# A transformer stack of two blocks on one core: small gate rows made later, context loaded later, queries and keys of the second block prepared apart, one gMLP input projected late

## The chip, the cores and the metric

The kernel runs on one core of a Trainium2 chip. TensorE multiplies, VectorE, ScalarE and GpSimd do the rest, SyncE issues the DMAs; the engines run side by side, each its own instructions in order, and wait for one another by semaphores. The metric is the device time in microseconds (us) from a launch to its end. GpSimd has next to no work in this kernel.

## The reference

All values are float32; `x` has 256 tokens of width 1024. `first_block` is one layer:

```python
h = rmsnorm(x, norm1_g)
(hg_q, hg_f, hg_i, hg_g, ml_qk, ml_v, ml_if, ml_o, mb_z, mb_xbc, mb_dt, gate_pre) = split(h @ w_in)
y_hg = rmsnorm(hgrn2_scan(silu(hg_q), log_f, hg_i)) * silu(hg_g)
qk   = silu(causal_dwconv(ml_qk, ml_conv_w, ml_conv_b))
y_ml = rmsnorm(mlstm_scan(q_m, k_m, ml_v, i_pre, log_sigmoid(ml_f))) * sigmoid(ml_o)
dt   = softplus(mb_dt + mb_dt_bias)
y_mb = rmsnorm((ssd_scan(xs, dt, A, Bm, Cm) + D * xs) * silu(mb_z))
x = x + (gates[0] * (y_hg @ w_hg) + gates[1] * (y_ml @ w_ml) + gates[2] * (y_mb @ w_mb)) @ w_out
u_g, u_v = split(causal_dwconv(rmsnorm(x) @ w_up, ffn_conv_w, ffn_conv_b))
x = rmsnorm(x + (silu(u_g) * u_v) @ w_down)
```

`second_block` has two layers, with a context `ctx` of 256 more tokens that the last layer only reads:

```python
sh1, sc1, g1, sh2, sc2, g2 = modulation(c, w_ada[i], b_ada[i])        # and the same for ctx
h  = rms_norm(x) * (1 + sc1) + sh1;   hc = the same of ctx
a_z, bq, bk, bv, cq, ck, cv = split_proj(h @ w_in[i])
u, v  = split(gelu(a_z));  out_a = u * (w_s @ rms_norm(v) + b_s)      # gated MLP over chunks of 128
out_b = window_attn(rope(rms_norm(bq)), rope(rms_norm(bk)), bv, keys and values of ctx, sink)
out_c = rms_norm(diff_attn(rope(rms_norm(cq)), rope(rms_norm(ck)), cv, keys and values of ctx))
x = x + g1 * (concat(out_a, out_b, out_c) @ w_out[i])
x = x + g2 * conv_ffn(rms_norm(x) * (1 + sc2) + sh2)
```

In layer 0 the context goes through the same steps (attention only to itself).

## The kernel before

**Weights.** Every float32 operand is split in two parts of the multiplier's format, high and low, and a product is three matmuls (high by high, high by low, low by high; `mm3`, L409). `weight` (L388) brings a weight tile of 128 x 1024 by DMA (`raw`, four buffers), ScalarE casts its high part (`wh`, L393) and VectorE subtracts the low part (`wl`, L395), three buffers each. `gemm_ws` (L422, tile `psg`) is then 24 matmuls of 128 x 256; `gemm_xs` (tile `psx`, L439 to 441) has the tokens as the stationary side, takes two weight tiles and does 24 matmuls for each block of 128 tokens.

**What sets the order.** The Python code only emits instructions. A scheduler with pools of buffers puts each engine's instructions in a row: in the order of the code where data and buffers allow it by its own estimate of times, else what is ready. Two streams of work are merged by generators: `run_ratio(a, b, n)` takes `n` steps of `b` for each step of `a`.

**First block.** After norm and split of `x`, `proj_a` projects the HGRN2 inputs; beside it `hgrn_core` works by chunks (tiles `hb`, `lnk`, `E`, `AT`, `psl`). `small_rows` (L782) makes softplus and its running sum for the SSD branch: an absolute value and an exponential on ScalarE, and 17 VectorE steps on 128 x 256 (a reciprocal, seven steps of a series at L796, a scan). It is called before `run_ratio(seq(pa, proj_b(), proj_c()), ...)`, with the load of `win` (the window mask, 256 KB) and its cast `winb` behind it. `proj_b` (L931) then runs eight `mqk` gemms, each with a convolution (ScalarE one tap, VectorE three, `cv`, L923) and a silu (`mq`), four pairs of `mv` weights, and more. The MLP `ffn` calls `hook1(j)` once per item `j`; from item 9 on it takes steps of `context_norm`: `prepare(0)` (load of layer 0's parameters `plt`, tables `ct...`, `st...` for the rotation) and the context's first norm. The modulation of layer 0 (`ada`, tiles `psada`, `arow`, `psat`) comes in quarters in between; `context_norm` first runs what is left of it.

**Second block.** `unit` (L1416) projects one input by name: `kv`, `ck` (keys, values), `cq`, `bq0`, `bq1` (queries), `cv` (values of the differential attention), `av` and `au` (the two inputs of the gated MLP; gelu on ScalarE at the evacuation). `qk_part(c)` (L1452) takes the two token blocks of `c` (0 is x, 1 the context): squares on ScalarE, sums on VectorE, Newton steps for the inverse root (`qny`, `qnt`), rotation (`rot`), scaling, then transposes on TensorE (`pst`) and the split into `qkh` and `qkl`. `attention(tiles, age)` (L1662) has eight items for each block of 128 tokens: four pairs of heads of the window kind, four of the differential kind. An item is scores (`psc`, three matmuls per head, 512 keys), maximum on VectorE, exponential on ScalarE (`Pp`), `age` items later the transposes (`psc<-ct,Pp`) and their copy (`PT`), one item after that the values (`pso`). Layer 1 does all projections first, then `gmlp(0)`, attention over blocks 1 and 0 with `age` 3, then `out_proj` (eight gemms over the eight k-tiles: 0, 1 from the gated MLP, 2 to 5 from the window heads, 6, 7 from the differential heads).

## Time and profile before

| | |
|---|---|
| runs before | 1729.18 us (median of 3: 1727.62 to 1729.49) |
| profiled run | 1728.11 us |
| its span, first to last instruction | 1726.3 us |
| mean granted clock of TensorE | 0.991 |
| TensorE busy | 1680.2 us (97%) |
| VectorE busy | 1422.8 us (82%) |
| ScalarE busy | 943.0 us (55%) |

The shares of busy time are means over stages with different limits, so stretches of 6 to 30 us are read one by one below. PE is TensorE's matmuls, PEld its weight loads (beside the matmuls), DVE VectorE, ACT ScalarE, SP SyncE. A row "PEld a <- DVE b" means that the weight load for `a` waited for `b`; the matmul behind it waits about as long. The overlap of neighbouring VectorE instructions (the next starts some 0.08 us before the last one's end) makes a row of them shorter than the sum of their durations.

### The profile page before, as it was taken

What the parts mean: (1) busy time and instruction counts of PE and PEld (TensorE: products, weight loads), DVE (VectorE), ACT (ScalarE), POOL (GpSimd) and SP (SyncE); (2) the same over time, 40 slices, a digit from 0 to 9 for tenths busy, and PEclk for the clock granted to TensorE, in tenths of its full rate; (3) what the DMA queues carried; (4) which work ended last, traced back from release to release, by engine and by line L of the source; (5) the groups of instructions that cost most, each with busy time, mean ns of one, the idle gap of its engine ahead of it and who ended that gap; (6) DMA issues with size and microseconds to landing.
All of it is one profiled execution on the core that took longest, in us unless ns stands there. A gap on an engine that the chain in (4) does not pass through costs nothing.

```text
span 1726.3 us, 31575 instructions
## 1 busy us (share of the span) xinstructions
PE 1680.2 (97%) x12334; PEld 1529.8 (89%) x12334; DVE 1422.8 (82%) x2788; ACT 943.0 (55%) x1661; POOL 0.2 (0%) x4
## 2 busy tenths in 40 slices
PE   7999999999999999999999999999999998899999
PEld 7999998889898999989877988888888996799999
DVE  8987977668789987876788899999997868688776
ACT  7655644444456665666777553431244555576454
POOL 0000000000000000000000000000000000000000
PEclk9999999999999999999999999999999999999999
DMA  8545454536665677764311546657753542046564
GB/s 264 162 151 156 137 159 121 150 111 213 206 212 165 194 234 224 218 203 147 99 50 52 169 138 184 186 170 237 242 165 110 170 134 63 1 144 196 177 193 135
DMA packets 80645, 278.01 MB, mean 161 GB/s; under 512 B 9072, under 2 KB 13808, under 8 KB 80240
## 3 DMA queue, kind: packets, MB, share of 16 engines
q1 hardware_dynamic: 80496, 275.99, 52.1%
q8 instruction: 97, 1.59, 0.4%
q14 instruction: 52, 0.43, 0.1%
HBM read 274.91 MB, written 1.05 MB: 160 GB/s over the span
## 4 chain that ended last, share of the span: by engine, by line
PE 84%; DVE 10%; ACT 3%; DMA 2%; issue 1%; SPq 0%; ACTq 0%; DVEq 0%
PE psg L414 20%; PE psg L417 20%; PE psg L416 20%; PE psx L439 3%; PE psx L441 3%; PE psx L440 3%; DVE wl L395 3%; PE psc L1568 2%; PE psl L894 1%; PE psc L1607 1%; ACT wh L393 1%; PE pso L1629 1%; PE pso L1626 1%; DMA raw<-w 1%; ACT Pp L1587 1%
## 5 line engine op out<-in xcount | busy, mean ns | idle before, releaser
L393 ACT CAST wh<-raw 128x1024 fp32r<-128x1024 f32 (+1 forms) x439 | 453.3, 1037 | 514.3 <-PE psg L416 419.0
L395 DVE TENSOR_TENSOR wl<-raw,wh 128x1024 fp32r<-128x1024 f32 (+1 forms) x439 | 528.2, 1206 | 136.6 <-ACT wh L393 133.6
L414 PE MATMUL psg<-XH,wh 128*128 128x256 f32 (+1 forms) x1272 | 396.3, 314 | 4.7 <-ACT wh L393 3.8
L417 PE MATMUL psg<-XH,wl 128*128 128x256 f32 (+1 forms) x1272 | 395.0, 313 | 4.7 <-DVE wl L395 4.7
L416 PE MATMUL psg<-XL,wh 128*128 128x256 f32 (+1 forms) x1224 | 384.6, 315 | 0.9 <-DVE XL L1331 0.5
L414 PEld LDWEIGHTS psg<-XH,wh 128*128 128x128 f32 x1272 | 240.3, 190 | 23.3 <-ACT wh L393 5.9
L417 PEld LDWEIGHTS psg<-XH,wl 128*128 128x128 f32 x1272 | 240.6, 190 | 21.3 <-DVE wl L395 5.7
L416 PEld LDWEIGHTS psg<-XL,wh 128*128 128x128 f32 x1224 | 231.9, 190 | 17.6 <-issue 1.1
L414 PE MATMUL psg<-xh,wh 128*128 128x256 f32 x720 | 208.2, 289 | 1.3 <-ACT xh L400 1.3
L417 PE MATMUL psg<-xh,wl 128*128 128x256 f32 x720 | 205.3, 285 | 2.6 <-DVE wl L395 2.6
L416 PE MATMUL psg<-xl,wh 128*128 128x256 f32 x720 | 205.7, 286 | 0.6 <-DVE xl L401 0.6
L414 PE MATMUL psg<-hh,wh 128*128 128x256 f32 (+1 forms) x592 | 178.6, 303 | 0.2
L416 PE MATMUL psg<-hl,wh 128*128 128x256 f32 (+1 forms) x592 | 178.3, 302 | 0.0
L417 PE MATMUL psg<-hh,wl 128*128 128x256 f32 (+1 forms) x592 | 178.2, 302 | 0.0
L414 PEld LDWEIGHTS psg<-xh,wh 128*128 128x128 f32 x720 | 137.8, 191 | 4.9 <-issue 2.9
L417 PEld LDWEIGHTS psg<-xh,wl 128*128 128x128 f32 x720 | 137.7, 191 | 4.9 <-DVE wl L395 3.2
L416 PEld LDWEIGHTS psg<-xl,wh 128*128 128x128 f32 x720 | 138.1, 192 | 1.8 <-issue 1.0
L414 PEld LDWEIGHTS psg<-hh,wh 128*128 128x128 f32 x592 | 111.0, 188 | 7.3 <-ACT hh L400 1.1
L416 PEld LDWEIGHTS psg<-hl,wh 128*128 128x128 f32 x592 | 111.2, 188 | 5.7 <-DVE hl L401 0.2
L417 PEld LDWEIGHTS psg<-hh,wl 128*128 128x128 f32 x592 | 111.1, 188 | 5.1
L439 PE MATMUL psx<-wh,XH 128*128 128x256 f32 x384 | 110.2, 287 | 1.3 <-ACT wh L393 0.8
L441 PE MATMUL psx<-wl,XH 128*128 128x256 f32 x384 | 109.3, 286 | 0.6 <-DVE wl L395 0.4
(445 smaller groups left out, 3181.7 us busy)
## 6 DMA issues: line engine op xcount, KB each, us to landing
raw<-w SPq DMA_DIRECT2D x238, 512.0 KB, 4.1
raw<-wb SPq DMA_DIRECT2D x197, 512.0 KB, 4.3
araw<-w SPq DMA_DIRECT2D x56, 512.0 KB, 4.3
raw<-w SPq DMA_DIRECT2D x16, 384.0 KB, 3.3
raw<-wb SPq DMA_DIRECT2D x8, 384.0 KB, 4.0
xres<-xT SPq DMA_DIRECT2D x16, 128.0 KB, 4.3
ccb<-pcb SPq DMA_DIRECT2D x2, 1024.0 KB, 5.4
plt<-pl SPq DMA_DIRECT2D x2, 588.0 KB, 4.2
```

Of the source, the lines that this page charges most:

```text
L393: S.copy(wh[:, 0:sz], raw[:, 0:sz])
L395: V.tensor_tensor(wl[:, 0:sz], raw[:, 0:sz], wh[:, 0:sz], ALU.subtract)
L414: T.matmul(o, wh[:, k], xh, start=(first and k == 0), stop=False)
L416: T.matmul(o, wh[:, k], xl, start=False, stop=False)
L417: T.matmul(o, wl[:, k], xh, start=False, stop=(last and not late and k == nk - 1))
L439: T.matmul(o, xh, wh[:, k % 4], start=(k == 0), stop=False)
L440: T.matmul(o, xl, wh[:, k % 4], start=False, stop=False)
L441: T.matmul(o, xh, wl[:, k % 4], start=False, stop=(k == 7))
L894: T.matmul(ps[:, a, t], E[:, o:o + 128], E[:, o:o + 128], start=True, stop=True)
L1568: T.matmul(ps[e][:, 0:A.nk], q_[d, jq, A.tq], k_[d, jk, kk], start=(n == 0), stop=(n == 2 and not mask))
L1587: S.activation(out=p[:, 0:A.nk], in_=o, func=AF.Exp, scale=ss[:, A.t, h:h + 1], bias=nm, accum_out=sums[:, c:c + 1])
L1607: T.transpose(ps[:, n], p[:, b * 128:(b + 1) * 128], ident)
```

## The change

- **Start.** `small_rows` is called in `proj_b` ahead of the fifth `mqk` gemm, with its rows in another pool. `win` is loaded and cast in two halves at items 6 and 7 of the first MLP. The second gate gemm's result is scaled after the norm's split.
- **Context.** `cx` is loaded at item 4 of the first MLP and the parameters of layer 0 at item 9, each held back by a small ScalarE copy from that item's `av`; a quarter of the modulation is taken at items 12, 15 and 18. In the first MLP's opening the weight of the next item is requested one step earlier.
- **Queries and keys.** `qk_part(c, which)` does the queries or the keys of `c`; sums, Newton steps and transposes are separate (the rows of `qkh` are in another order, so that the transposes of a part are together). Layer 0 takes keys first. Layer 1 takes x's queries, then the context's keys, then x's keys; its first four steps run during `kv` and `ck`.
- **gMLP of layer 1.** `av` is copied out and gets its gelu in one instruction afterwards. The `au` gemms, their gelu and the product come in `gmlp(0, late=True)`, whose steps are taken at items 1, 3, 5, 14, 16 and 17 of attention, which runs with `age` 2. `out_proj` takes its k-tiles in the order 2, 3, 4, 5, 0, 1, 6, 7 in both layers.

```diff
+    fill2 = (1, 3, 5, 14, 16, 17)
...
-    def load_params(pool, spec, src, nm):
+    def load_params(pool, spec, src, nm, gate=None):
...
+        if gate is not None:
+            S.copy(t[:, 0:1], gate[:, 0:1])
         nc.sync.dma_start(out=t, in_=src)
...
-                    hook(j)
+                    hook(j, av)
...
-    uf = [scaled(gemm_ws(0, ("hf", j), graw, 256)) for j in range(2)]
+    uf = [gemm_ws(0, ("hf", j), graw, 256) for j in range(2)]
+    uf[0] = scaled(uf[0])
     normed(xh, xl, x, r, g1[:, 0:8])
+    uf[1] = scaled(uf[1])
...
     def proj_b():
         for j in range(8):
+            if j == 4:
+                small_rows()
...
-    small_rows()
     V.tensor_copy(identb, ident)
     V.tensor_copy(causb, C("causal"))
-    win = mid.tile([128, 512], F32, tag="E", name="win", bufs=4)
-    nc.sync.dma_start(out=win, in_=cstw)
-    V.tensor_copy(winb.rearrange("p a b -> p (a b)"), win)
...
-    cx = load_x(res2, ctxT, tag="cx")
+    cx = res2.tile([128, 8, 256], F32, name="xres", tag="cx")
...
-    def hook1(j):
+    def hook1(j, av):
+
+        gate[0] = av
+        if j in (6, 7):
+            win = tmp.tile([128, 256], F32, tag="t256", name="win", bufs=6)
+            nc.sync.dma_start(out=win, in_=cstw[:, (j - 6) * 256:(j - 5) * 256])
+            V.tensor_copy(winb[:, j - 6], win)
+        if j == 4:
+            S.copy(cx[:, :, 0:1], av[:, 0:8].unsqueeze(2))
+            for k in range(8):
+                nc.sync.dma_start(out=cx[:, k], in_=ctxT[:, k])
         if j >= 9:
             next(cn, None)
+        if j in (12, 15, 18):
+            ada_steps(1)
...
+        QKPART = {"q": (((0, 512, 64), (640, 896, 32)), (((0, 1, 2, 3), 0), ((5, 6), 4))),
+                  "k": (((512, 640, 64), (896, 1152, 32)), (((4, 7, 8), 6),))}
+
+        def qk_part(c, which):
...
+        def gelu(c, which=(0, 1)):
+
+            for a in (A[c][e] for e in which):
+                S.activation(out=a, in_=a, func=AF.Gelu_apprx_tanh)
...
+            if late:
+                for j in range(2):
+                    ps = gemm_ws(ph, ("au", j), lambda k: (XH[:, k, XS], XL[:, k, XS]), 256)
+                    S.copy(AU[:, j], ps[:, 0:256])
+                    yield
+                for _ in gelu(c, (1,)):
+                    pass
+                for b in range(2):
+                    gated(b)
                 yield
...
-                ps = gemm_ws(ph, ("out", m), lambda k: (XH[:, k, o], XL[:, k, o]), 256)
+                ps = gemm_ws(ph, ("out", m), lambda k: (XH[:, k, o], XL[:, k, o]), 256, ks=[2, 3, 4, 5, 0, 1, 6, 7])
...
-            for _ in units(("kv", "ck"), 0, 1):
-                pass
-            run_ratio(seq(units(("av", "au"), 0), units(("cv",), 0, 1)), seq(qk_part(0), qk_part(1)), Knobs.rc)
+
+            qk = seq(qk_part(0, "q"), qk_part(1, "k"), qk_part(0, "k"))
+            run_ratio(units(("kv", "ck"), 0, 1), (next(qk) for _ in range(4)), 2)
+            run_ratio(seq(units(("av",), 0), gelu(0, (0,)), units(("cv",), 0, 1)), qk, Knobs.rc)
             psum(c=6, o=1, s=1)
-            for _ in seq(gmlp(0), attention((1, 0), 3)):
+            gm = gmlp(0, True)
+            for i, _ in enumerate(attention((1, 0), 2)):
+                if i in Knobs.fill2:
+                    next(gm, None)
+            for _ in gm:
                 pass
```

Line numbers move by 4 to 62 (before's L393, L395, L923 are L397, L399, L931 after the change). Three places of the engines' rows:

VectorE in the mLSTM projection, around the `wl` of the first `mv` gemm, before (the first and the last row are the `wl` of the last `mqk` gemm and of the first `mv` gemm):

```order
L395 TENSOR_TENSOR wl<-raw,wh 128x1024
L837 SCALAR_TENSOR_TENSOR mq<-th,cv 128x256
L923 SCALAR_TENSOR_TENSOR cv<-psg,pb1t,cv 128x253
L886 TENSOR_TENSOR E<-E,hq 128x64x4
L923 SCALAR_TENSOR_TENSOR cv<-psg,pb1t,cv 128x254
L884 TENSOR_TENSOR E<-hb 128x128x2
L923 SCALAR_TENSOR_TENSOR cv<-psg,pb1t,cv 128x255
L901 COPY_PREDICATED AT<-ct_125,psl 128x2x256
L923 SCALAR_TENSOR_TENSOR cv<-psg,pb1t,cv 128x253
L837 SCALAR_TENSOR_TENSOR mq<-th,cv 128x256
L923 SCALAR_TENSOR_TENSOR cv<-psg,pb1t,cv 128x254
L395 TENSOR_TENSOR wl<-raw,wh 128x1024
```

After, the last 12 rows ahead of that `wl` (the last row here; the `wl` before it stands 25 rows above the first of these):

```order
L931 SCALAR_TENSOR_TENSOR cv<-psg,pb1t,cv 128x254
L805 SCALAR_TENSOR_TENSOR p<-p,s 128x256
L931 SCALAR_TENSOR_TENSOR cv<-psg,pb1t,cv 128x255
L807 SCALAR_TENSOR_TENSOR SP<-p,z 128x256
L909 COPY_PREDICATED AT<-ct_125,psl 128x2x256
L808 TENSOR_SCALAR z<-SP,acol 128x256
L845 SCALAR_TENSOR_TENSOR mq<-th,cv 128x256
L809 SCALAR_TENSOR_TENSOR CS<-ct_125,z 128x256
L931 SCALAR_TENSOR_TENSOR cv<-psg,pb1t,cv 128x253
L894 TENSOR_TENSOR E<-E,hq 128x64x4
L931 SCALAR_TENSOR_TENSOR cv<-psg,pb1t,cv 128x254
L399 TENSOR_TENSOR wl<-raw,wh 128x1024
```

The small-gate rows (L798 to L809) now stand between the convolution taps, and 35 instructions lie between the two `wl` where there were 10.

TensorE at the end of layer 1's attention, before: scores, transposes and values of the last items, then the output projection (`psg`):

```order
L1568 MATMUL psc<-qkh 128x512 x2
L1568 MATMUL psc<-qkl,qkh 128x512 x2
L1568 MATMUL psc<-qkh,qkl 128x512 x2
L1607 MATMUL psc<-ct,Pp 128x128 x8
L1629 MATMUL pso<-CV,PT 128x128 x12
L1607 MATMUL psc<-ct,Pp 128x128 x4
L1629 MATMUL pso<-CV,PT 128x128 x4
L414 MATMUL psg<-XH,wh 128x256
```

After, at the same place; `psg` is here an `au` gemm:

```order
L421 MATMUL psg<-XL,wh 128x256
L422 MATMUL psg<-XH,wl 128x256
L1664 MATMUL psc<-ct,Pp 128x128 x4
L1686 MATMUL pso<-CV,PT 128x128 x4
L1625 MATMUL psc<-qkl,qkh 128x512 x2
L1625 MATMUL psc<-qkh,qkl 128x512 x2
L419 MATMUL psg<-XH,wh 128x256
L421 MATMUL psg<-XL,wh 128x256
L422 MATMUL psg<-XH,wl 128x256
L1686 MATMUL pso<-CV,PT 128x128 x4
L419 MATMUL psg<-XH,wh 128x256
```

The 48 matmuls of the `au` gemms now stand among the last transposes and values.

ScalarE there, before (up to the squares of the differential heads' output):

```order
L1587 ACTIVATE Pp,dsums<-psc,dnm,ss 128x512 x2
L1643 COPY rsb<-psrs 128x512
L1612 COPY PT<-psc 128x512 x2
L400 CAST XH<-rsb 128x4x128
L1587 ACTIVATE Pp,dsums<-psc,dnm,ss 128x512 x2
L1612 COPY PT<-psc 128x512
L1654 ACTIVATE sqc<-OB 128x256
```

After:

```order
L1669 COPY PT<-psc 128x512
L1644 ACTIVATE Pp,dsums<-psc,dnm,ssq 128x512 x2
L1669 COPY PT<-psc 128x512
L397 CAST wh<-raw 128x1024
L1589 COPY AU<-psg 128x256
L1669 COPY PT<-psc 128x512
L1543 ACT_TABLE_LOAD
L1543 ACTIVATE AU<-AU 128x512
L1711 ACTIVATE sqc<-OB 128x256
L404 CAST XH<-oa 128x256 x2
```

Two weight casts, the copies of the `au` results, a table load and the gelu now stand among the last copies and ahead of the squares.

## Rows read from the trace of the kernel before

**Rows 1.** The page, busy time, the chain that ended last, one costly group

```profile
PE 1680.2 (97%) x12334; PEld 1529.8 (89%) x12334; DVE 1422.8 (82%) x2788; ACT 943.0 (55%) x1661; POOL 0.2 (0%) x4
...
PE 84%; DVE 10%; ACT 3%; DMA 2%; issue 1%; SPq 0%; ACTq 0%; DVEq 0%
...
L395 DVE TENSOR_TENSOR wl<-raw,wh 128x1024 fp32r<-128x1024 f32 (+1 forms) x439 | 528.2, 1206 | 136.6 <-ACT wh L393 133.6
```

**Rows 2.** Stretches: length, busy us (PE, PEld, DVE, ACT, POOL), granted clock, DMA share, GB/s

```profile
100.00:125.00 25.00, 25.00 (x213) 24.90 (x212) 22.52 (x44) 14.73 (x27) 0.00 (x0) 1.00 0.49 148
738.00:752.00 14.00, 11.80 (x64) 7.12 (x64) 9.93 (x19) 11.39 (x20) 0.00 (x0) 0.92 0.75 247
1372.00:1400.00 28.00, 27.77 (x232) 27.60 (x233) 17.08 (x34) 14.55 (x31) 0.00 (x0) 1.00 0.50 151
1430.00:1446.00 16.00, 12.32 (x105) 11.00 (x103) 13.79 (x46) 6.54 (x15) 0.00 (x0) 1.00 0.50 150
1446.00:1475.00 29.00, 26.69 (x208) 18.10 (x210) 20.78 (x58) 18.97 (x43) 0.00 (x0) 0.88 0.01 2
1500.00:1512.00 12.00, 9.11 (x61) 8.51 (x60) 4.95 (x20) 2.90 (x8) 0.00 (x0) 0.86 0.00 0
```

**Rows 3.** Waits, 20 to 30 us: engine, line, releaser, total, times, longest

```profile
PEld psg L417 <- DVE wl L395: 1.6, 1, 1.6
```

**Rows 4.** Waits, 50 to 58 us

```profile
PEld psl L869 <- DVE hq L837: 1.7, 1, 1.7
...
DVE winb L1214 <- DMA win<-cstw: 0.7, 1, 0.7
```

**Rows 5.** Groups of VectorE, 0 to 60 us: count, busy, mean ns, idle before

```profile
L796 DVE SCALAR_TENSOR_TENSOR p<-p,s 128x256 f32<-128x256 f32 x7 | 3.0, 424 | 0.2
...
L791 DVE RECIPROCAL s<-s 128x256 f32<-128x256 f32 x1 | 1.7, 1736 | 0.0
```

**Rows 6.** Timeline of VectorE, mLSTM projection: start, duration, line, tile, shape

```profile
118.57 1.22 DVE L395 TENSOR_TENSOR wl<-raw,wh 128x1024 fp32r<-128x1024 f32 x1
...
123.35 0.48 DVE L923 SCALAR_TENSOR_TENSOR cv<-psg,pb1t,cv 128x254 f32<-128x254 f32 x1
123.75 1.22 DVE L395 TENSOR_TENSOR wl<-raw,wh 128x1024 fp32r<-128x1024 f32 x1
```

**Rows 7.** Timeline of TensorE, first `mv` gemm

```profile
129.44 0.28 PE L441 MATMUL psx<-wl,xh 128*128 128x256 f32 x1
```

**Rows 8.** Waits, 540 to 546 us

```profile
PEld psg L417 <- DVE wl L395: 3.2, 1, 3.2
```

**Rows 9.** Waits, 594 to 605 us

```profile
PEld psg L417 <- DVE wl L395: 1.6, 2, 1.1
```

**Rows 10.** Waits, 738 to 748 us

```profile
PEld psat L538 <- ACT arow L563: 1.9, 1, 1.9
...
PEld psx L439 <- ACT wh L393: 1.4, 1, 1.4
```

**Rows 11.** Waits, 880 to 888 us

```profile
PEld psg L414 <- ACT wh L393: 2.4, 1, 2.4
...
PEld psc L1607 <- DVE Pp L1596: 0.9, 1, 0.9
```

**Rows 12.** Waits, 1436 to 1447 us

```profile
PEld pst L1500 <- DVE qkl L401: 3.1, 3, 1.3
...
PEld psc L1568 <- DVE qkl L401: 1.2, 1, 1.2
```

**Rows 13.** Waits, 1494 to 1506 us

```profile
PE psc L1607 <- DVE Pp L1596: 2.2, 1, 2.2
...
PEld pso L1629 <- ACT PT L1612: 0.9, 1, 0.9
```

**Rows 14.** Timeline of ScalarE, first exponentials of layer 1

```profile
1449.61 1.28 ACT L1587 ACT_TABLE_LOAD   x1 [3.93 <-DVE nm L1585]
1450.90 0.78 ACT L1587 ACTIVATE Pp<-psc,nm,ss 128x512 f32<-128x512 f32 x1
```

More of the change, by code (lines that the diff above doesn't have):

```diff
@@ L407, in gained, with mm3 @@
             V.scalar_tensor_tensor(dst_l[:, k], x[:, k], g[:, k:k + 1], dst_h[:, k], ALU.mult, ALU.subtract)
-    def mm3(o, w, rhs, nk, late=False, first=True, last=True):
+    def mm3(o, w, rhs, nk, late=False, first=True, last=True, ks=None):
         wh, wl = w
-        for k in range(nk):
+        ks = ks or list(range(nk))
+        for k in ks:
             xh, xl = rhs(k)
-            T.matmul(o, wh[:, k], xh, start=(first and k == 0), stop=False)
+            T.matmul(o, wh[:, k], xh, start=(first and k == ks[0]), stop=False)
             if not late:
                 T.matmul(o, wh[:, k], xl, start=False, stop=False)
-            T.matmul(o, wl[:, k], xh, start=False, stop=(last and not late and k == nk - 1))
+            T.matmul(o, wl[:, k], xh, start=False, stop=(last and not late and k == ks[-1]))
         if late:
@@ L662, in ffn @@
                         ps.append(gemm_ws(ph, ("up",) + k, raw[0], raw[3]))
+                    ahead = weight(ph, ("up", raws, 0), 128)
                     us += [raw[1](p) for p in ps[len(us):]]
@@ L678, in ffn @@
                 else:
-                    pg = gemm_ws(ph, ("up", j, 0), part(slice(0, n)), n)
+                    pg = gemm_ws(ph, ("up", j, 0), part(slice(0, n)), n, w=ahead if raw and j == raws else None)
                 ag = conv(pg, j, "ag")
@@ L769, in tile_two_blocks @@
     S.activation(out=lbe, in_=lbe, func=AF.Exp)
+    S.activation(out=sg0, in_=ones, func=AF.Sigmoid)
     lbs = p1.tile([128, 8], F32, name="lbs")
@@ L1346, in context_norm @@
         ada_steps(max(0, 32 - Ada.done))
-        LS[0] = prepare(0)
+        LS[0] = prepare(0, gate[0])
         yield
@@ L1437, in unit @@
                     for i, c in enumerate(cs):
-                        S.activation(out=A[c][1][:, j], in_=ps[:, 256 * i:256 * i + 256], func=AF.Gelu_apprx_tanh)
+                        S.activation(out=A[c][1][:, j], in_=ps[:, 256 * i:256 * i + 256], func=AF.Copy if last else AF.Gelu_apprx_tanh)
                 return
@@ L1441, in unit @@
                     "cv": lambda t, o: S.copy(CV[:, t], o),
-                    "av": lambda t, o: S.activation(out=A[t // 2][0][:, t % 2], in_=o, func=AF.Gelu_apprx_tanh)}[nm]
+                    "av": lambda t, o: S.activation(out=A[t // 2][0][:, t % 2], in_=o, func=AF.Copy if last else AF.Gelu_apprx_tanh)}[nm]
             key = ("bq", int(nm[2])) if nm[:2] == "bq" else (nm,)
@@ L1449, in units @@
                 yield
-        def qk_part(c):
+        QKPART = {"q": (((0, 512, 64), (640, 896, 32)), (((0, 1, 2, 3), 0), ((5, 6), 4))),
+                  "k": (((512, 640, 64), (896, 1152, 32)), (((4, 7, 8), 6),))}
+        def qk_part(c, which):
             toks = (2 * c, 2 * c + 1)
-            full = not (last and c)
+            groups, moves = QKPART[which]
+            ss = S_[which][:, 2 * c:2 * c + 2]
+            n0 = (groups[0][1] - groups[0][0]) // 64
             for t in toks:
-                for c0, c1, d, g0 in (((0, 512, 64, 0), (512, 640, 64, 8), (640, 1152, 32, 10)) if full
-                                      else ((512, 640, 64, 8), (896, 1152, 32, 18))):
+                g0 = 0
+                for c0, c1, d in groups:
                     sq = ap.tile([128, 512], F32, tag="scr", name="sq", bufs=Knobs.scr)
@@ L1496, in qk_part @@
                     g0 += nh
-                for j0, j1 in (((0, 4), (4, 8), (8, 9)) if full else ((4, 5), (7, 9))):
+                if t < 2:
+                    yield
+                for js, to in moves:
+                    n = len(js)
                     ps = PS.s.tile([128, 4, 128], F32, tag="s", name="pst")
-                    for j in range(j0, j1):
-                        T.transpose(ps[:, j - j0], QK[t][:, j * 128:(j + 1) * 128], ident)
-                    split(qkh[:, j0:j1, t * 128:(t + 1) * 128], qkl[:, j0:j1, t * 128:(t + 1) * 128], ps[:, 0:j1 - j0])
+                    for i, j in enumerate(js):
+                        T.transpose(ps[:, i], QK[t][:, j * 128:(j + 1) * 128], ident)
+                    split(qkh[:, to:to + n, t * 128:(t + 1) * 128], qkl[:, to:to + n, t * 128:(t + 1) * 128],
+                          ps[:, 0:n])
@@ L1557, in scores @@
                     d = slice(64 * e, 64 * e + 64)
-                    rows.append((d, i, 4, 2 * i + e, L.nsink[:, 2 * i + e:2 * i + e + 1]))
+                    rows.append((d, i, 6, 2 * i + e, L.nsink[:, 2 * i + e:2 * i + e + 1]))
                 else:
@@ L1577, in scores @@
             for e, (d, jq, jk, h, nsink) in enumerate(rows):
-                c = h if i < 4 else h - 10
+                c = h if i < 4 else h - 8
                 o, nm = ps[e][:, 0:A.nk], nmt[:, c:c + 1]
```

102 lines of the change are left out of this document (56 added, 46 removed).

## The prediction

> **What bounds the kernel now.** I read the page first. TensorE is busy 97% of the span of 1726.3 us and holds 84% of the chain that ended last, VectorE 10% [rows 1]: the time changes only where TensorE stops, or goes on at half clock. Then I listed, for each stretch that the diff touches, which waits TensorE has there and what ended them. Almost all end on VectorE: the low half of a weight, `wl` (439 subtractions, 1.21 us each), or a chain of small vector steps that queued in front of one. A stretch at full speed holds 213 matmuls in 25 us, 0.117 us each, so a gemm of 24 is 2.8 us [rows 1, 2]. A second loss is the clock: where the granted clock of a stretch is below 1, part of it ran at the lower of the two levels (1.2 instead of 2.4 GHz), after TensorE had waited. Its price is the missing share times the length: 0.12 x 29 = 3.5 us in 1446 to 1475, 0.14 x 12 = 1.7 us in 1500 to 1512, 0.08 x 14 = 1.1 us in 738 to 752 [rows 2].
>
> The profiled run took 1728.11 us, 1.07 below the median of 1729.18. The sum is made against the profiled run, and 1.1 us is put back at the end.
>
> **Start (0 to 58 us).** The small-gate rows and the window mask's load and cast leave this place. In front of the third gate gemm TensorE waited 1.6 us for `wl`, whose subtraction now stands earlier in VectorE's row; at 51.5 us it waited 1.7 us for `hq`, which stood behind the cast `winb`, itself held 0.7 us by the mask's DMA [rows 3, 4]. The first wait goes wholly. Of the second I take half, since ScalarE's chain for the same chunk is late next: -1.6 - 0.9 and 0.2 for the shorter row, **-2.7**, between -1.6 (the first alone) and -3.3 (both).
>
> **The small-gate rows in the mLSTM projection (117 to 140 us).** They cost what they cost before: a reciprocal of 1.74 us, seven steps of 0.42 us, nine more of 0.2 to 0.7 us [rows 5], some 7 us of VectorE where instructions overlap by 0.08. But they now stand in front of a weight. Before, the `wl` for the last `mqk` gemm starts at 118.57 and the one for the first `mv` gemm at 123.75; TensorE needs the latter at 129.44 [rows 6, 7], so there are 4.5 us in hand. In the new order 35 instructions stand between these two: the small rows (6.9 us), 11 convolution taps (0.48 us, the next starts after 0.40: 4.4), and seven others (`mq`, `E`, two masked copies) of 2.9 us by the same reading, together 14.2. The second `wl` would start at 118.6 + 1.1 + 14.2 = 133.9 and end at 135.1, 5.7 us after TensorE wants it. VectorE is busy 22.5 of 25 us here [rows 2], so nothing else can give way. Behind this wait in TensorE's row stand all of `mv` and the HGRN2 chunks. I take **+6.0**. If the taps are spread out differently it is +3; if the clock drops too, as it does in the three stretches of [rows 2] after such waits, 1.7 more: +3 to +8.
>
> **Entry of the first MLP.** The rotary tables of layer 0 no longer stand between the Newton steps of the norm, where TensorE's longest wait for `wl` is 3.2 us [rows 8]. They are ten steps on at most 128 columns, about 1 us by my estimate: **-1.0** (0 to -3.2). The context rows arrive later and nobody waits for them.
>
> **Inside the first MLP (594 to 605 us).** Parameters of layer 0 are now loaded at item 9, so the tables and the norm's sums stand together between two `wl`. By the durations of the same steps in this trace I estimate 9.8 us of VectorE without one; the gemms use a `wl` every 2.8 us, and the three buffers hold a lead of at most 3 x 2.8 = 8.4. TensorE already waited 1.6 us here for `wl` [rows 9]. I take **+2.5** (0 if the lead holds, +4.5 if it is gone).
>
> **End of the first MLP (738 to 752 us).** Three of the modulation's quarters move into items 12, 15 and 18, between gemms. Before, they stood in a block with nothing beside them: TensorE waited 1.9 us for the transposed row and 1.4 us for the next weight [rows 10], and lost 1.1 us by the clock [rows 2], 4.4 in all. Two quarters remain there: **-3.0** (-1 to -4.4). The moved quarters cost their own matmuls in either place.
>
> **Layer 0's attention.** Keys now come before queries, and the two `au` gemms and the first output gemms move ahead of the queries' transposes. TensorE's waits for a weight cast (2.4 us, ScalarE had table loads in front of it) and for `Pp` (0.9 us) [rows 11] go, but the transposes of the queries then wait for a chain of about as much VectorE work. **0**, between -3.3 and +3.3.
>
> **Layer 1.** Before, VectorE idles 10.9 of 28 us in 1372 to 1400 and then is busy 13.8 of 16 us in 1430 to 1446 [rows 2], where TensorE waits 3.1 us for the transposed keys and 1.2 us more before the first score [rows 12]. The queries' share of the steps, by my estimate 8 us (norm, rotation and scaling of two token blocks), moves into the idle stretch. But the two `au` gemms, 2 x 2.8 us, leave the projections too, so TensorE comes to the keys 5.6 us sooner; of the 4.3 us only **-1** is gained. The `au` gemms go where TensorE had nothing: 2.2 us waiting for `Pp` and 0.9 us for `PT` at the end of attention [rows 13], **-3.1**, and then the output projection starts at full clock, **-1.7**. New there is a chain from the second `au` gemm to the output projection: copy 0.4, table load 1.28, gelu on 512 columns (0.78 is the nearest row, an exponential of that shape) [rows 14], product, cast and difference 0.4 each: 3.7 us, beside the last values (1 us) and the 12 matmuls on other k-tiles that the new k order puts first (1.4), so 1.3 us stand out: **+1.3**. At the start of attention I take half of the 3.5 us that the clock cost, **-1.7**, and **+0.2** for the shorter lag between scores and values (age 2). Together **-6.0**, from +1 (the waits come back in new places) to -11.
>
> The added table load can be weighed against a page. Here the load takes 1.28 us and the exponential starts 0.01 us behind it [rows 14]. The Trainium skill, "ScalarE: Activation LUTs", section "What ACT_TABLE_LOAD costs", gives about the same for the load but adds a drain of 1380 ns to each switch, and its rules for kernel authors say to do all of one table set before switching; this change does the gelu of the two halves apart. By the page the tail would be 1.4 us longer than in my sum; the trace shows no such drain.
>
> **Sum.** -2.7 + 6.0 - 1.0 + 2.5 - 3.0 + 0 - 6.0 = -4.2: 1728.1 - 4.2 = 1723.9, and with the 1.1 us to the median 1725.0.
>
> **Rivals.** *The small rows are hidden:* VectorE's row is as long, but the `wl` of `mv` comes in time, as 4.5 us in hand and TensorE's HGRN2 matmuls would allow if half of the 14.2 us lay behind it. Then +6 becomes +2: 1721. For it: the scheduler that set the order keeps a `wl` ahead of its gemm almost everywhere. Against: the order itself has 35 instructions in between. Chance 0.22. *The `au` gemms are only moved:* what is saved at the end of attention is lost before its start, because TensorE now reaches the keys before VectorE has them. Layer 1 then gives -1 instead of -6: 1730. For it: VectorE's 13.8 of 16 us. Chance 0.14. *Slower:* the wait in `mv` is the full 5.7 us plus 1 us for the second weight half, and the clock falls behind it (5.7 + 1 + 1.7 = +8.4, its place 129 to 140 us); with -1 at the end of the MLP and -2 in layer 1 the sum is -2.7 + 8.4 - 1 + 2.5 - 1 - 2 = +4.2: 1732.3, with the 1.1 us 1733. It decides once layer 1 gives less than 2.5 us. Chance 0.15. *The table switch costs more:* if ScalarE is held at the load in the tail for as long again as the load itself takes (1.28 us [rows 14]), layer 1 gives -4.7 and the time is 1726.3. In the row no gap follows the load, so 0.03. This is the rule of the page named above.
>
> **How the numbers follow.** My forecast has 0.46, with a range of its own from 1721 to 1729. The measurement tells 0.2% from no change, 3.5 us: faster means below 1725.7. The forecast lies across this border, 0.28 below it and 0.18 above. Faster: 0.28 + 0.22 = 0.50. Same: 0.18 + 0.14 + 0.03 = 0.35. Slower: 0.15. The range goes from the hidden rows with a better layer 1 (1721 - 5 = 1716) to the slower rival (1733) and 1 more.
>
> **What would show it.** Right: a wait of TensorE for `wl` of 4 to 8 us near 129 us; no wait of over 1 us at the end of layer 1's attention, `psg` matmuls between the last `pso`; a full clock at its output projection; at 50 us no wait for `hq` of over 1 us. Wrong: `mv` starts without a wait; the keys' transposes in layer 1 wait longer than 4 us; or a wait of over 2 us in layer 0's attention before its first scores, which my zero there does not hold.

## The result and the profile after

The changed kernel takes **1743.58 us** (1741.10 to 1749.61), the kernel before 1728.40 beside it: the ratio is **1.0093, interval [1.0074, 1.0111]**, some 15 us slower. The prediction was 1725.0, with a range from 1716 to 1734: wrong in size and in sign.

The page of the kernel after, busy time and the chain that ended last:

```profile
PE 1681.0 (97%) x12334; PEld 1526.3 (88%) x12334; DVE 1425.3 (82%) x2818; ACT 946.5 (54%) x1672; POOL 0.2 (0%) x4
...
PE 54%; DVE 6%; ACT 2%; issue 1%; DMA 0%; DVEq 0%; ACTq 0%; SPq 0%
```

Against [rows 1] busy times are the same within 4 us; the 15 us are time in which TensorE stops or runs at half clock. Stretches of the kernel after (length, busy us of PE, PEld, DVE, ACT, POOL, granted clock, DMA share, GB/s):

```profile
125.00:140.00 15.00, 10.74 (x70) 10.32 (x69) 13.38 (x27) 4.38 (x8) 0.00 (x0) 0.77 0.30 96
...
568.00:622.00 54.00, 49.07 (x370) 46.85 (x369) 48.09 (x114) 35.17 (x63) 0.00 (x0) 0.94 0.66 206
...
750.00:778.00 28.00, 22.35 (x148) 21.05 (x147) 20.51 (x54) 16.37 (x35) 0.00 (x0) 0.82 0.41 144
...
880.00:900.00 20.00, 16.24 (x114) 13.94 (x115) 13.22 (x42) 18.49 (x34) 0.00 (x0) 0.85 0.07 19
900.00:920.00 20.00, 15.55 (x101) 12.57 (x100) 18.42 (x59) 9.21 (x16) 0.00 (x0) 0.89 0.31 96
...
1450.00:1466.00 16.00, 13.30 (x98) 10.33 (x97) 13.88 (x41) 6.24 (x12) 0.00 (x0) 0.89 0.31 98
1500.00:1516.00 16.00, 15.03 (x144) 11.76 (x144) 12.63 (x34) 10.75 (x25) 0.00 (x0) 1.00 0.00 1
```

The same work in the kernel before (its layer 0 runs some 10 us earlier on the clock):

```profile
125.00:140.00 15.00, 15.00 (x131) 15.00 (x131) 14.25 (x29) 8.97 (x18) 0.00 (x0) 1.00 0.51 147
...
568.00:622.00 54.00, 52.25 (x429) 50.64 (x428) 52.11 (x111) 37.03 (x61) 0.00 (x0) 1.00 0.63 194
...
872.00:892.00 20.00, 16.10 (x113) 13.02 (x112) 16.90 (x55) 17.60 (x36) 0.00 (x0) 0.91 0.15 50
892.00:912.00 20.00, 19.85 (x153) 14.11 (x154) 17.53 (x57) 11.85 (x29) 0.00 (x0) 1.00 0.18 54
```

In the kernel after, TensorE waits in each of the first six stretches, and runs below full clock behind the waits. Three of them, 125 to 140, 568 to 622 and 900 to 920 us, had a clock of 1.00 before. The other three, the end of the MLP (738 to 752 us in [rows 2]), 880 to 900 us and the start of layer 1's attention, had waits and a clock below 1 before too. In 900 to 920 us TensorE is busy 15.6 us where it was busy 19.9, and VectorE is busy 18.4.

To see where the time goes I laid the start times of the 10,192 weight matmuls (`psg`, `psx`) of both traces side by side, the n-th of one against the n-th of the other. The lead or lag of the kernel after, which is then charged to a stage by its growth:

| up to | lag in us | of this stage | predicted |
|---|---|---|---|
| 118 us (start) | -2.2 | -2.2 | -2.7 |
| 152 us (small-gate rows) | +5.0 | +7.2 | +6.0 |
| 567 us (rest of the first block, entry of the MLP) | 0.0 | -5.0 | -1.0 |
| 630 us (inside the first MLP) | +7.7 | +7.6 | +2.5 |
| 843 us (its end, entry of layer 0) | +12.0 | +4.3 | -3.0 |
| 991 us (layer 0's attention) | +21.9 | +9.9 | 0 |
| 1378 us | +23.2 | +1.3 | 0 |
| 1536 us (layer 1 up to its output projection) | +16.5 | -6.7 | -6.0 |
| end | +14.4 | -2.1 | 0 |

One trace against one trace carries the chance of both: half-clock stretches of different length behind comparable waits (last section). So each stage was priced by experiments. TensorE's waits in the kernel after (engine, tile, line, releaser, total us, times, longest; "issue" is time in which the engine waited for nothing that the profile shows):

```profile
PEld psl L877 <- DVE hq L845: 0.8, 1, 0.8
...
PE psl L902 <- DVE E L894: 2.4, 1, 2.4
PE psx L444 <- DVE cv L931: 1.9, 1, 1.9
...
PEld psg L422 <- DVE wl L399: 3.2, 1, 3.2
...
PEld psg L422 <- DVE wl L399: 1.8, 1, 1.8
...
PEld psr L497 <- DVE rcy L466: 2.4, 1, 2.4
PEld psg L419 <- ACT hh L404: 1.1, 1, 1.1
...
PEld psn L480 <- DVE sacc L488: 2.3, 1, 2.3
...
PEld psx L446 <- DVE wl L399: 2.9, 1, 2.9
...
PEld pso L1686 <- ACT PT L1669: 3.6, 1, 3.6
...
PEld pst L1530 <- issue: 1.9, 1, 1.9
PEld psg L419 <- ACT AU L1457: 1.8, 1, 1.8
PEld pst L1530 <- DVE qkl L405: 1.4, 1, 1.4
...
PEld pst L1530 <- DVE qkl L405: 2.8, 1, 2.8
...
PEld psg L419 <- ACT rsb L1700: 0.8, 1, 0.8
```

They stand, in this order, at 50 to 58 us ([rows 4]: 1.7 has become 0.8), 124 to 133 (small-gate rows), 541 to 547 ([rows 8], unchanged), 576 to 582 and 600 to 612 (inside the first MLP, [rows 9]), 750 to 758 and 766 to 773 (its end, [rows 10]), 888 to 897 and 900 to 916 (layer 0's attention, [rows 11]), 1452 to 1462 (layer 1, [rows 12]) and 1495 to 1520 (its end, [rows 13]: 2.2 has become 0.8).

### The profile page after: what moved, and what is told of

Same layout as the page of the kernel before. It is cut to its first block, busy times and chain, and to the rows that moved or that the text cites. A ratio compares the mean times of both kernels' runs of the same rounds, so it can differ in the third digit from the quotient of the medians.

```text
span 1740.7 us, 31642 instructions
## 1 busy us (share of the span) xinstructions
PE 1681.0 (97%) x12334; PEld 1526.3 (88%) x12334; DVE 1425.3 (82%) x2818; ACT 946.5 (54%) x1672; POOL 0.2 (0%) x4
## 4 chain that ended last, share of the span: by engine, by line
PE 54%; DVE 6%; ACT 2%; issue 1%; DMA 0%; DVEq 0%; ACTq 0%; SPq 0%
PE psg L419 13%; PE psg L422 13%; PE psg L421 13%; PE psx L444 2%; PE psx L446 2%; PE psx L445 2%; PE psc L1625 2%; PE psc L1664 1%; PE pso L1686 1%; DVE wl L399 1%; DVE mx L1638 1%; PE pso L1683 1%; ACT wh L397 1%; ACT Pp L1644 1%; DVE h L1335 1%
## 5 line engine op out<-in xcount | busy, mean ns | idle before, releaser
L397 ACT CAST wh<-raw 128x1024 fp32r<-128x1024 f32 (+1 forms) x439 | 453.7, 1038 | 515.0 <-PE psg L421 416.0
L399 DVE TENSOR_TENSOR wl<-raw,wh 128x1024 fp32r<-128x1024 f32 (+1 forms) x439 | 527.9, 1206 | 130.0 <-ACT wh L397 126.3
```

Of the source, the lines that this page charges most:

```text
L397: S.copy(wh[:, 0:sz], raw[:, 0:sz])
L399: V.tensor_tensor(wl[:, 0:sz], raw[:, 0:sz], wh[:, 0:sz], ALU.subtract)
```

## The experiments

Each kernel was compared with the kernel before beside it. A price is the difference of two such ratios times 1728 us. With intervals of 0.13 to 0.3% on either side it holds to some 4 to 6 us, and a smaller price is not told from zero by the ratios alone; the difference of medians is given too where the two disagree. The last two columns split the mean time of a kernel's runs: the clock's part is the missing share of the mean granted clock times the span, the rest is the remainder (in the first row over all runs of the kernel before that stood beside an experiment). The split is rough, as a half-clock stretch costs nothing where TensorE would have waited.

| kernel | median us | ratio to before [interval] | clock | rest |
|---|---|---|---|---|
| before | 1728.4 | 1 | 17.1 | 1710.7 |
| after | 1743.6 | 1.0093 [1.0074, 1.0111] | 26.1 | 1718.3 |
| e1 layer 0 together | 1731.8 | 1.0021 [1.0007, 1.0036] | 22.5 | 1710.0 |
| e2 inserts undone | 1736.4 | 1.0037 [1.0024, 1.0050] | 20.5 | 1715.9 |
| e3 rows at start | 1740.2 | 1.0067 [1.0038, 1.0096] | 25.6 | 1715.5 |
| e4 layer 1 alone | 1722.8 | 0.9964 [0.9949, 0.9980] | 13.3 | 1709.2 |
| e5 layer 0, 8 steps | 1740.1 | 1.0067 [1.0052, 1.0082] | 26.1 | 1713.7 |
| e6 context early | 1746.1 | 1.0101 [1.0071, 1.0131] | 28.3 | 1717.3 |
| e7 parameters ungated | 1748.3 | 1.0113 [1.0091, 1.0135] | 30.6 | 1717.3 |
| e8 quarters at end | 1743.8 | 1.0091 [1.0073, 1.0110] | 25.3 | 1718.7 |
| e12 e6 and e7 | 1744.1 | 1.0100 [1.0082, 1.0118] | 27.6 | 1716.2 |
| e9 layer 0 apart, early | 1735.7 | 1.0058 [1.0036, 1.0080] | 23.4 | 1712.8 |
| e10 e1 and e2 | 1724.0 | 0.9983 [0.9968, 0.9998] | 17.5 | 1706.6 |
| **e11 e10 and rows at start** | **1718.1** | **0.9953 [0.9935, 0.9971]** | 14.6 | 1703.8 |
| e13 e11 + context late | 1718.7 | 0.9944 [0.9922, 0.9966] | 13.7 | 1705.0 |
| e14 e11 + gated parameters | 1719.7 | 0.9950 [0.9932, 0.9967] | 16.2 | 1703.7 |
| e15 e11 + quarters | 1723.2 | 0.9973 [0.9955, 0.9992] | 18.9 | 1704.6 |
| e17 e11 + context, parameters | 1723.9 | 0.9970 [0.9957, 0.9983] | 16.9 | 1706.5 |
| e16 e11 + layer 0 apart, early | 1721.1 | 0.9962 [0.9943, 0.9980] | 15.1 | 1706.6 |
| e18 e11, layer 1's au early | 1719.6 | 0.9944 [0.9925, 0.9964] | 13.5 | 1705.1 |

Lines in the experiments' kernels stand 18 to 90 below those of the kernel after.

**e1: layer 0 prepares queries and keys together** (`qk_old` is `qk_part` of the kernel before).

```diff
-            run_ratio(seq(units(("av", "au"), 1), units(("cv",), 0, 1)), seq(qk_part(1, "k"), qk_part(1, "q")), 8)
+            run_ratio(seq(units(("av", "au"), 1), units(("cv",), 0, 1)), qk_old(1), 8)
...
-            run_ratio(seq(units(("new", "kv", "ck", "cq", "bq0", "bq1"), 0), qk_part(0, "k"), qk_part(0, "q")),
+            run_ratio(seq(units(("new", "kv", "ck", "cq", "bq0", "bq1"), 0), qk_old(0)),
                       seq(gmlp(1), attention((3, 2), 2)), Knobs.ra)
```

> The kernel after, but layer 0 prepares queries and keys together again, as before (layer 1 keeps them apart). Theory A (the loss lies in layer 0's attention, where the trace after drifts by +10 us against the trace before between 846 and 990 us): 10 us less than after, 1733.5 (1730.5 to 1736.5). Theory B (my forecast's terms: layer 0 is neutral, the small-gate rows ahead of the first mv weight carry the loss): 1743.5, within 3.

It took 1731.8 us: 12.4 less than after by the ratios, 11.8 by the medians. In the alignment of start times e1 is within 0.9 us of the kernel after up to 843 us, and gains 10.5 us between 843 and 991: the price lies where the edit is. Its two stretches that answer to 880 to 920 above:

```profile
880.00:900.00 20.00, 16.53 (x117) 13.04 (x116) 16.13 (x52) 19.19 (x41) 0.00 (x0) 0.91 0.09 27
900.00:920.00 20.00, 19.60 (x152) 14.18 (x151) 18.27 (x58) 10.88 (x28) 0.00 (x0) 1.00 0.26 81
```

TensorE is busy 19.6 us again in the second, as before. The term that I had put at zero came out as the largest single price.

**e5 and e9: how late the queries start.** In the merge of `run_ratio`, each step of the projections and of the preparation takes two of the 24 steps of the context's gated MLP and attention. Six steps are the projections; with one combined part behind them the queries' squares come after 6 x 2 = 12 of the 24 (the expectations say 13); with keys first, five steps more, after 22. e5 takes away the extra step between rotation and transposes (18 of 24); e9 does that too, emits both parts' squares and Newton steps in one step (12 of 24) and keeps the rest apart:

```diff
-                if t < 2:
+                if t < 2 and last:
                     yield
...
+        def both(k, q):
+            next(k)
+            next(q)
+            yield
+            yield from k
+            yield from q
```

> The kernel after, but in layer 0 the preparation of x's queries and keys is cut into 8 steps instead of 12 (the step between rotation and transposes goes), so that the queries' squares are emitted after 18 of the 24 steps of the context's gated MLP and attention instead of after 22 (with both together, as before: 13). Theory A (the queries start so late that TensorE has run out of the context's attention when VectorE begins with them): part of the 12 us comes back, 5 less than after, 1739 (1734 to 1741). Theory B (keeping them apart costs by itself, two Newton chains and more small steps): 1743.5, within 2.

> The kernel after, with layer 0's queries and keys still apart, but the squares and Newton steps of both emitted in one step, after 13 of the 24 steps of the context's gated MLP and attention, where the kernel before has them; 8 steps in all. Theory A (the lateness of the queries is the loss): 10 less than after, 1733.5 (1730 to 1736). Theory B (keeping them apart is the loss, lateness only the 4 us that the kernel with 8 steps gave back): 1739.5 (1737 to 1742).

e5 gives back 4.5 us (3.5 by the medians), e9 6.0 (7.9). In the alignment, the stage from 843 to 991 us costs 9.9 us in the kernel after, 5.5 in e5, 5.3 in e9 and -0.6 in e1. So the lateness is about half of the price, or more; e5 and e9 are not told apart. What happens is read from ScalarE and VectorE of the kernel after (start, duration, engine, line, [idle before <- releaser]):

```profile
890.92 0.48 ACT L404 CAST qkh<-pst 128x384 fp32r<-128x384 f32 x1
891.42 1.28 ACT L1457 ACT_TABLE_LOAD   x1
892.71 0.38 ACT L1457 ACTIVATE AU<-psg 128x256 f32<-128x256 f32 x1
893.11 1.28 ACT L1644 ACT_TABLE_LOAD   x1
894.41 0.56 ACT L1644 ACTIVATE Pp<-psc,dnm,ssq 128x256 f32<-128x256 f32 x1
...
894.97 0.36 ACT L1669 COPY PT<-psc 128x256 f32<-128x256 f32 x1
...
895.10 0.17 DVE L1650 RECIPROCAL rc<-dsums 128x2 f32<-128x2 f32 x1 [2.99 <-ACT Pp L1644]
...
899.71 0.61 ACT L1484 ACTIVATE sq<-QK 128x512 f32<-128x512 f32 x1
```

The last items of the context's attention go through ScalarE one by one, with two table loads between them (gelu for `AU`, back to the exponential). TensorE waits 3.6 us, and VectorE idles 3.0 us, since the queries' steps, which could fill it, are emitted behind: their first square runs at 899.71. Then VectorE has 18.4 us of work in 20, and TensorE waits 1.8, 1.4 and 1.9 us. The two table loads, and a wait of TensorE behind them (2.4 us in [rows 11]), were there before too. But there VectorE rotated the queries meanwhile, as these rows of the kernel before show:

```profile
880.24 1.28 ACT L1438 ACT_TABLE_LOAD   x1
881.99 0.68 DVE L1494 TENSOR_TENSOR QK<-QK,ctbqn 128x512 f32<-128x512 f32 x1
882.48 1.28 ACT L1587 ACT_TABLE_LOAD   x1
882.80 0.68 DVE L1495 TENSOR_TENSOR QK<-QK,rot 128x512 f32<-128x512 f32 x1
```

In e9, with the squares early, no wait of TensorE between 880 and 900 us is over 0.5 us. The Trainium skill, "ScalarE: Activation LUTs", section "Rules for kernel authors", says to do all of one table set before switching; here ScalarE switches there and back around one gelu of 0.38 us, with loads of 1.28 us each by the rows.

e9 and e1 still differ by 4 us in the medians (6.4 by the ratios), so keeping the parts apart seemed to cost something itself.

**e16: apart, without the lateness**, on the kernel e11 (below).

> The same base of 1718.1, and layer 0's queries and keys apart again, with the squares and Newton steps of both at the place of the kernel before. Theory A (lateness was all of it): 1718, within 2. Theory B (apart costs by itself, two Newton chains and the rotations in two rounds, as 4 us were left over in the kernel after): 4 more, 1722 (1720.5 to 1725).

It costs 1.6 us by the ratios, 3.0 by the medians, and 2.8 in the column without the clock, as between e1 and e9 (2.8). That is Theory B, weakly: the ratio alone doesn't exclude zero. The rest of the 4 to 6 us between e9 and e1 stays open; e9's trace lost 6.8 us by the clock there (last section). In e9 the wait that is left (`pst`, L1567) stands in front of the queries' transposes:

```profile
PEld pst L1567 <- issue: 2.9, 2, 2.7
```

**e2, e6, e7, e8, e12: the first MLP's inserts.** e2 undoes all three, e6 the context, e7 the gate, e8 the quarters, e12 the context and the gate:

```diff
-    cx = res2.tile([128, 8, 256], F32, name="xres", tag="cx")
+    cx = load_x(res2, ctxT, tag="cx")
...
-        LS[0] = prepare(0, gate[0])
+        LS[0] = prepare(0)
...
-        if j == 4:
-            S.copy(cx[:, :, 0:1], av[:, 0:8].unsqueeze(2))
-            for k in range(8):
-                nc.sync.dma_start(out=cx[:, k], in_=ctxT[:, k])
...
-        if j in (12, 15, 18):
-            ada_steps(1)
```

> The kernel after, but the context is loaded early again, layer 0's parameters are loaded without waiting for item 9, and no quarters of the modulation are taken at items 12, 15 and 18 of the first MLP. Theory A (these inserts stop TensorE by some 8 to 12 us between 567 and 800 us: context DMAs ahead of a weight 3.5, parameters and tables 3.4, quarters and a late entry of layer 0 2 to 5): 1733.5 (1731 to 1737). Theory B (forecast: inside +2.5, end -3, so the whole is worth nothing): 1744.

> The kernel after, but the context is loaded early as before, not at item 4 of the first MLP. Theory A (the eight context DMAs go ahead of a weight in SyncE's row, which costs a wait of 1.77 us for wl at 578 us and a half-clock stretch of 3.4 us, 1.7): 3.5 less than after, 1740 (1738 to 1742). Theory B (a wait here is made up by the next one): 1743.5, within 1.5.

> The kernel after, but the load of layer 0's parameters does not wait for item 9 (no ScalarE copy ahead of it). Theory A (the tables then stand between other steps earlier, and the waits of 2.4 and 1.1 us at 605 us shrink to the one wait of the kernel before): 3 less than after, 1740.5 (1738.5 to 1742.5). Theory B (the tables are taken at item 9 in any case): 1743.5, within 1.5.

> The kernel after, but no quarters of the modulation are taken at items 12, 15 and 18; they stand at the end of the first MLP as before. Theory A (trace of the kernel with all three inserts undone: 3.2 us less inside the MLP, hardly more at its end): 3 less than after, 1740.5 (1738 to 1742). Theory B (the forecast's term of -3 for moving them is real): 3 more than after, 1746.5.

> The kernel after, with the context loaded early and layer 0's parameters not gated, but the quarters of the modulation still at items 12, 15 and 18. Theory A (each insert costs what its traces show locally, 1.6 and 4.9 us between 555 and 620 us, and the clock's chance lengths hid it in the single runs): 6.5 less than after, 1737 (1735 to 1740). Theory B (only all three together cost anything, the quarters being the one that decides): 1743.5, within 2.

All three together give back 9.7 us by the ratios (7.2 by the medians). One alone, or the two of e12, give back nothing that can be told from zero: by the ratios e6, e8 and e12 stand within 2 us of after, e7 3.5 above it. My Theory A missed in all four, although the waits went as expected: in e7 and e12 those of 2.4 and 1.1 us at 605 us are gone. The columns show where it lies: without the clock's part, e12 is 2.1 us better than after and e2 2.4, but the clock's part is 27.6 in e12 and 20.5 in e2.

**e13, e14, e15, e17: each insert put on the kernel without the others** (e11).

> The kernel with layer 0 together, no inserts and the small-gate rows at the start (1718.1), and one insert put back: the context loaded at item 4 of the first MLP. Theory A (its wait for wl of 1.77 us and one half-clock stretch more): 2.5 more, 1720.5 (1719 to 1723). Theory B (free by itself, as taking it away from the kernel after brought nothing): 1718, within 1.5.

> The same base of 1718.1, and only the gated load of layer 0's parameters put back. Theory A (the waits of 2.4 and 1.1 us at 605 us in place of two of 1.0, and a half-clock stretch): 3.5 more, 1721.5 (1720 to 1724). Theory B (free by itself): 1718, within 1.5.

> The same base of 1718.1, and only the quarters of the modulation at items 12, 15 and 18 put back. Theory A (at the end of the MLP waits of 2.4 and 2.9 us in place of 1.5 and 1.0, and longer half-clock stretches; traces with and without differ by 5 us between 640 and 850 us): 5 more, 1723 (1721 to 1726). Forecast's term: 3 less, 1715.

> The base of 1718.1 (layer 0 together, no inserts, small-gate rows at the start), with the context load at item 4 and the gated parameters put back together, quarters at the end. Theory A (the inserts cost the same wherever they are put, 0.5 and 1.5 us alone): 1720, within 2. Theory B (the two load the same stretch from 565 to 615 us and cost more together, as the kernel after with the quarters undone lost 7.5 us against that with all three undone): 1725 (1723 to 1727).

Context and gated parameters cost nothing alone that can be told (-1.6 and -0.5 us by the ratios, 0.5 and 1.6 by the medians), the two together 2.9 (5.8 by the medians), the quarters 3.5 (5.1). So the gain of 3.0 us that I had put on moving the quarters is not there; what was measured has the other sign, though the ratio alone does not exclude zero. TensorE's waits at the end of the MLP, 730 to 765 us, with the quarters moved (e15), then without (e11):

```profile
PEld psx L464 <- DVE wl L417: 2.9, 1, 2.9
PEld psx L462 <- ACT wh L415: 1.3, 1, 1.3
PEld psat L561 <- ACT arow L586: 1.0, 1, 1.0
```

```profile
PEld psat L561 <- ACT arow L586: 1.9, 1, 1.9
PEld psx L462 <- ACT wh L415: 1.4, 1, 1.4
PEld psx L464 <- DVE wl L417: 0.6, 1, 0.6
```

Moving the quarters takes 0.9 us from the wait for the transposed row and adds 2.3 to that for the weight of layer 0's first projection. My reading is that with fewer quarters TensorE gets there sooner, and VectorE, with the norm of x in front of that `wl`, does not. The clock adds more than the waits: in 736 to 778 us it is 0.84 in e15 and 0.96 in e11, 5.0 us of 42. In e17 the stretch from 574 to 608 us has the same waits as the kernel after: 2.4 us (`psr` for `rcy`), 1.7 (`wl`), 1.1 (`hh`).

What stays open: why undoing the quarters alone (e8), or the other two alone (e12), brings nothing in the kernel after while all three bring 7 to 10 us. The last column gives 1.2 - 0.1 + 0.8 = 1.9 us for e13 to e15 against e11, near the 2.4 of e2 against after, but 2.7 for e17, where its two parts alone give 1.1. The clock's part does not add up either, and it was not settled what keeps it.

**e3, e10, e11: small-gate rows, and the best version.** e3 is the kernel after, e10 has e1 and e2 together, e11 is e10 with

```diff
     def proj_b():
         for j in range(8):
-            if j == 4:
-                small_rows()
...
     next(pa)
+    small_rows()
     V.tensor_copy(identb, ident)
```

> The kernel after, but the small-gate rows are made at the start again. Theory A (the drift of +7 us at 130 us is given back by 440 us, where other work was late anyway): 1743.5, within 2.5 (the start would lose 1 to 2 again). Theory B (the forecast's term of +6 stays to the end): 1737.5, 3 to 8 less than after.

> The kernel after, with layer 0's queries and keys together and all three inserts of the first MLP undone; the small-gate rows stay in the mLSTM projection. If the parts add up (start -2, small-gate rows +4, layer 1 -6 on the kernel before): 4 less than before, 1724 (1721 to 1727). If the parts hide one another (a wait removed comes back at the next place): 1728 or more.

> The same as the kernel with both undone, and the small-gate rows at the start again: what is left of the change is the start, the window mask and layer 1. If the parts add up: 4 less than that kernel, 1720 (1717.5 to 1722.5). If the wait in the mLSTM projection is given back later: no less than it, 1724.

The rows' new place costs 4.5 us on the kernel after (3.3 by the medians; this ratio has the wide interval of e3 and does not exclude zero) and 5.2 on e10 (5.9); without the clock's part 2.8 both times. In e3 TensorE is busy for the whole of 125 to 140 us, at a clock of 1.00. My reading of the lag, that it is given back by 440 us, is false: in the alignment with the kernel before, e3 gains there too, from 1.2 us ahead at 152 us to 5.8 at 440, and e3 and e11 stay ahead. e10 came out as the parts added up, 1724.0, and **e11 with 1718.1 is faster than both kernels**, 0.5% under the kernel before. What it keeps of the change is more than the expectation says: the start, the window mask, the weight requested a step earlier, layer 0's k-tile order, an added sigmoid on ScalarE at the start, and layer 1.

**e4 and e18: layer 1.** e4 is the kernel before with layer 1's part of the diff. e18 is e11 with the `au` gemms back among the projections:

```diff
-            run_ratio(seq(units(("av",), 0), gelu(0, (0,)), units(("cv",), 0, 1)), qk, Knobs.rc)
+            run_ratio(seq(units(("av", "au"), 0), gelu(0), units(("cv",), 0, 1)), qk, Knobs.rc)
...
-            gm = gmlp(0, True)
+            gm = gmlp(0)
```

> The kernel before with layer 1's part of the change alone (queries and keys apart, late au, k-tile order of its output projection). Theory A (forecast's term and the drift between the traces, -6.8 us from 1360 us on): 6 to 7 us less than before, 1721.5 (1719 to 1724). Rival (the au gemms are only moved): 1 us less, 1727.5.

> The same base of 1718.1, but layer 1's au gemms stand in the projections again (queries and keys apart, gelu after the copy and age 2 stay). Theory A (forecast's terms for the tail: waits of 3.1 us and one half-clock stretch of 1.7 come back, the chain of 1.3 goes): 3.5 more, 1721.5 (1720 to 1724). Theory B (what is lost at the tail is won at the start of attention, where the wait for the keys, 2.7 us and its half-clock stretch, goes because TensorE comes 5.6 us later): 1718, within 1.5.

Layer 1's part gives 6.2 us (5.5 by the medians), some 5 of it in the clock's part (13.3; its own runs of the kernel before had 18.3). No part of it was found in the late `au` gemms: e18 stands 1.6 us below e11 by the ratios and 1.5 above by the medians. The waits change places. With `au` early (e18), 1428 to 1450 us has no wait for the keys, and the end of attention, 1485 to 1500, has these:

```profile
PEld pso L1776 <- ACT PT L1759: 2.2, 3, 0.9
PEld pso L1776 <- issue: 2.0, 1, 2.0
PEld psc L1754 <- DVE Pp L1743: 1.2, 1, 1.2
```

With `au` late (e11) the start of attention has one wait of its length, and the end hardly any:

```profile
PEld pst L1567 <- DVE qkl L423: 2.7, 1, 2.7
...
PEld psg L437 <- ACT rsb L1790: 0.8, 1, 0.8
PEld pso L1776 <- ACT PT L1759: 0.6, 1, 0.6
```

## Why the prediction was wrong, by its own steps

**Start, -2.7: right.** The lag is -2.2 at 118 us, the wait of 1.6 us for `wl` [rows 3] is gone, and the wait for `hq` is 0.8 us where it was 1.7. With the rows back at the start (e3) the lag there is still -1.2, so about half of this term came from their leaving.

**Small-gate rows, +6.0 (+3 to +8): right in size.** The lag is +7.2, the price 3 to 6 us. The mechanism was right in part (the rows stand between the taps, TensorE comes to a stop near 129 us, then the clock: 0.23 x 15 = 3.4 us), but the wait named, 4 to 8 us for `wl`, was not: TensorE stopped for a convolution tap and for `E`, 1.9 and 2.4 us, which stand between the same rows, before it came to the weight, whose `wl` started at 131.4 and not 133.9. The rival that hides the rows is out.

**Entry of the first MLP, -1.0: no gain.** The wait is 3.2 us as in [rows 8], though the tables have left; they were not what held that `wl`. The -5.0 of the table's third row is something else: e3 gains 2.8 us between 152 and 567 us too, and what it is was not tested.

**Inside the first MLP, +2.5 (0 to +4.5): at its upper end.** The waits are 1.8, 2.4 and 1.1 us where [rows 9] has 1.6 in all, and the clock gives 0.06 x 54 = 3.2 us. Context and parameters together cost 3 to 6 us, and neither alone a price that can be told.

**End of the first MLP, -3.0: wrong sign.** A failed step is "4.4 in all", of which 3.0 should go. I priced the waits that the quarters caused and not what stood behind them, VectorE's norm ahead of layer 0's first weight: that wait grew from 0.6 to 2.9 us, and the clock fell more. Quarters alone: +3.5 to +5.

**Layer 0's attention, 0 (+-3.3): the step that failed most.** The price is +12.4. I balanced the waits of [rows 11] against a chain of "about as much VectorE work" and counted instructions; I did not count emission steps. The change turns 7 steps into 12 in a merge that takes two attention steps per step, so the work that should have covered the queries' chain was spent by the time the chain began. This lateness is 6 to 8 us of the price by e9; keeping the parts apart adds 2 to 3 by e16, and the rest is open. The sign that I had written down, a wait of over 2 us before the first scores of x, came: 3.6 us, then 1.8, 1.4 and 1.9. The range of 3.3 was made from the waits of the old trace, where that cover was still in place.

**Layer 1, -6.0: right in total (-6.2), for partly wrong reasons.** The late `au` gemms, -3.1 and -1.7 in my sum, give nothing net that can be told, as the rival of the moved gemms had it: they bring a wait of 2.7 us at the start. So the gain has to come from what else the part does: the queries' earlier steps, the gelu apart from the evacuation, `age` 2, the k-tile order (not told apart). Much of it came through the clock: the two stretches of [rows 2] lost 0.12 x 29 + 0.14 x 12 = 5.2 us, those of the kernel after 0.11 x 16 = 1.8. The signs for the end came as written: no wait between 1495 and 1520 us is over 0.8 us, `au` matmuls stand between the last values, and the output projection starts at full clock.

**The table load: right.** At the end of layer 1's attention in the kernel after, the gelu starts 0.02 us behind the load of 1.28 us:

```profile
1521.61 1.28 ACT L1543 ACT_TABLE_LOAD   x1
1522.91 0.63 ACT L1543 ACTIVATE AU<-AU 128x512 f32<-128x512 f32 x1
```

The drain of about 1380 ns that the Trainium skill, "ScalarE: Activation LUTs", section "What ACT_TABLE_LOAD costs", adds to each switch is not in this trace, so the rival of the dearer table switch is out.

**The rival on the slower side** named a wait of `mv`; a wait is there, but it would have given 1733. What carried the rest were two terms whose cover I hadn't named (layer 0 and the quarters), the pair of context and parameters, and the clock: its part rose from 17 to 26 us, more than half of the loss. My sum only took clock losses off, 1.1 us at the end of the MLP and 1.7 twice in layer 1; a new loss of 1.7 us stood in one term's range and in this rival alone.

Together, by the ratios: start -1.2 (the trace of e3, as the price of the rows holds the rest), rows +4.5, inserts +9.7, layer 0 +12.4, layer 1 -6.2, in sum +19.2 against 15 to 16 measured, which is within what such prices hold to. As the prices were taken on different kernels and the inserts don't add up, the sum proves little.

## What to carry to other kernels

Where two generators are merged at a fixed ratio, cutting one of them into more steps is a change of the schedule: count how far the other has run when each chain starts, and what is left of it to cover the chain. A block of work that seems to cause a wait may also cover one; before pricing its removal, find what the engine behind it will then need, and when the other engines will have it. Price an added wait with the clock stretch that follows it, and test a part on its own base: parts that share a bound can each look free when only one of them is undone.
